# Four microseconds of products between the steps of three delta net lanes in a one-core decoder layer kernel

## The chip, the core and the metric

The kernel runs on one core of one Trainium2 chip. The metric is the device time of one execution, in microseconds (us). Times of a kernel come from a few runs; the profile comes from one execution more.

## What is computed

One layer of a hybrid decoder for 1024 prompt tokens and, with the same weights, 8 x 4 sample tokens, all in float32. A combined projection of the normalised input feeds three branches (sliding-window attention, a short gated convolution, a gated delta net); each branch is projected, gated and summed, and a gated MLP with a convolution follows. The change touches the delta net:

```
q, k = l2norm(q) * dk ** -0.5, l2norm(k)
beta, g = sigmoid(b), -exp(A_log) * softplus(a + dt_bias)
...
a_low = where(strict, (k * beta) @ k.T * decay, 0)
sol = triangular_solve(I + a_low, [v * beta, k * beta * exp(gc)])
qk = q @ k.T * decay
...
v_new = u - w @ S
o = (q * exp(gc)) @ S + qk @ v_new
S = S * exp(glast) + (k * exp(glast - gc)).T @ v_new
```

## The kernel before, in words

**The main line.** The work of TensorE (PE) that matters most is a fixed sequence of jobs of large matmuls, here called products. A projection job takes one block of 128 output columns: for each of three groups of tokens 24 products of 352 columns (`products`, L324), weights and activations split in a high and a low part. An `mm` tile (three PSUM banks in turn) takes each group, and an eviction on ACT or DVE (L1202, L1229, L1252, L1464) frees it. Later jobs are pairs of blocks that share fewer multiplications (`Pairs.run`, L1428, products of 264 columns); the first of them are the gate pairs, G16 and those behind it. Numbers of products in this document count the products in PE's order from the start.

**The lanes.** All else (norms, attention, delta net, their loads and stores) is written as generators, the lanes of class `Lanes` (L84 to L140). Every two to four products the main line calls `tick()`, which moves the clock of the planner by 0.36 to 0.45 us and runs one step of the first lane that is ready. A lane ends a step with a `yield`. A bare `yield` makes it ready at the next turn; `yield bg.after(us)` makes it ready when that many microseconds of products have been emitted; `bg.arrived()` waits for the planned end of its loads. So a lane's `yield` sets how many products stand on PE between a step that computes an operand (on DVE, ACT or POOL) and the matmul that reads it. Afterwards the Tile scheduler puts the instructions of each engine in order by its priorities. Each engine works through its own queue in that order.

**The delta net's lanes.** `pass1` (three lanes share the 8 chunks, L766 to L816) loads a chunk's rows, forms the decay on DVE (L784), ACT and POOL, multiplies on PE (L795) and evicts on DVE (L801, L802). When all chunks are done two lanes start. `solve` inverts the diagonal blocks with 31 pairs of DVE instructions (L827, L829) and a copy (L833); `merge` (L846 to L935) joins the blocks with tiny matmuls (L871, L880 of 32 columns) and lets `prep` and `scan` (L964 to L1011) run over the chunks. `sample_delta` (L1018 to L1126) does the sample group at one go: matmuls L1050, L1057, transposes L1062 to L1064, L1072, L1076, then 32 matmuls L1083 of 8 columns; the evictions L1058, L1059 lie on DVE.

**The gate pairs.** `h_build` (L1811, L1823 on DVE, L1811 on POOL, and splits in a high and a low part by L216 on ACT and L217 on DVE or POOL) makes the combined activations that the gate pairs multiply. Its gate for these is one line, `done.get("prep", 0) == NB and done.get("att", 0) >= HSTART`: all chunks prepared and most of the attention done. It works in four quarters; each product of a combined piece reads all four. `out_norm` (L604, L612) follows the scan.

Of the kernel before, what the change touches and what calls it, by code (L numbers as in the profile page):

```python
# [153 lines left out]
RAWGAP, SUMGAP = 5.0, 10.0  # L154
GAHEAD, GADD, GLO = 4, (), ()
# [14 lines left out]
STEP, EXP, BLKWAIT, PTWAIT, EXP2 = 1.0, 3.0, 4.0, 2.7, 1.0  # L170


def trunk(tc, A, O, cst_d):
    nc = tc.nc
    bg = Lanes()
# [22 lines left out]
    def banks(n):  # L198

        return lambda: held[0] + n <= limit[0]  # L200

    def keep(n):
        held[0] += n
        return [bg_ps() for _ in range(n)]
# [565 lines left out]
    def pass1(c):  # L770
# [18 lines left out]
        yield  # L789
        for hp in range(2):  # L790
            yield banks(1)
            ps, = keep(1)
            for i in range(2):
                h = hp * 2 + i
                mm(ps[:, i * 256:(i + 1) * 256], kn[:, h, :], kq[:, h, :, :].rearrange("p s t -> p (s t)"),  # L795
                   start=True, stop=True)
            yield bg.after(STEP)
            held[0] -= 1
            pv = ps.rearrange("p (h s t) -> p h s t", h=2, s=2)
            hs = slice(hp * 2, hp * 2 + 2)  # L800
            nc.vector.tensor_tensor(At[:, hs, :], pv[:, :, 0, :], Dt[:, hs, :], op=ALU.mult)  # L801
            nc.vector.tensor_tensor(qk[:, hs, :], pv[:, :, 1, :], qk[:, hs, :], op=ALU.mult)  # L802
            yield
# [37 lines left out]
    def merge():  # L841
# [25 lines left out]
        yield bg.arrived()  # L867
        yield banks(1)
# [7 lines left out]
        yield bg.after(1.8)  # L876
# [32 lines left out]
        yield there  # L909
        for i in range(2):  # L910
            yield banks(1)
            ps, = keep(1)
            for g in range(8):
                mm(ps[:, g * 64:g * 64 + 64], A64[i][:, g, :], X64[:, 8 * i + g, :], start=True, stop=True)
                if g % 4 == 3:
                    yield
            held[0] -= 1
            for hh in range(2):
                r = slice(64 * hh, 64 * hh + 64)
                nc.scalar.mul(W64[i][r, :, r], ps[r, :].rearrange("p (g j) -> p g j", j=64), -1.0)  # L920
            yield
# [101 lines left out]
    def sample_delta():  # L1023
# [24 lines left out]
        yield  # L1048
# [6 lines left out]
        yield  # L1055
# [4 lines left out]
        yield  # L1060
# [13 lines left out]
        yield  # L1074
# [18 lines left out]
        yield  # L1093
# [3 lines left out]
        yield  # L1097
# [5 lines left out]
        yield  # L1103
# [1314 lines left out]
```

## Time and profile before

| | us |
|---|---|
| runs, in order | 1893.98, 1896.81, 1889.29 |
| median | 1893.98 |
| profiled execution, its own time | 1890.09 |
| span of that execution | 1888.0 |
| mean granted clock of TensorE in it | 0.968 of full |

The span is the stretch from the first to the last instruction of the profiled execution; the execution's own time is 2.1 us longer. The granted clock is the share of full speed that the chip gave TensorE over the span.

### The profile page before, as it was taken

Reading aid. Unit: us, or ns where it says so; the run is one execution under the profiler, and the core shown is the slowest. Engines: PE = TensorE matmul, PEld = TensorE weight load, DVE = VectorE, ACT = ScalarE, POOL = GpSimd, SP = SyncE. Lnnn points to the kernel's source line nnn. Section 1 sums busy time; section 2 is a strip of 40 time slices with the busy share of each in tenths; the row PEclk is TensorE's granted clock in tenths of the full one; section 3 lists DMA queues with packets and bytes.
Section 4 is the critical chain, followed back from the end, with each engine's and each line's share of the span. In section 5 each row is a group of like instructions: output and inputs, shape, how many; then the busy total and the mean of one; then the engine's idle time right before and its main releaser. Section 6 shows DMA issues by size and latency. Waiting matters only on the chain.

```text
span 1888.0 us, 33612 instructions
## 1 busy us (share of the span) xinstructions
PE 1781.3 (94%) x12862; PEld 1741.7 (92%) x12862; DVE 1127.3 (60%) x1944; ACT 778.3 (41%) x1626; POOL 1061.4 (56%) x985
## 2 busy tenths in 40 slices
PE   5899999898999997999999999999999999899997
PEld 3799988798999996999999999999999999899997
DVE  5578823354478779431234766777777787764324
ACT  5444522221245433444321345445545544454433
POOL 3345534334333329986447246988998988344542
PEclk8899999997999997999999999999999999999999
DMA  6312597656566533553464344444444442695513
GB/s 220 104 47 80 180 301 219 173 154 147 154 163 168 153 104 110 198 207 112 166 223 142 121 137 148 142 153 156 161 147 153 144 161 98 239 369 185 178 48 108
DMA packets 299633, 300.79 MB, mean 159 GB/s; under 512 B 56708, under 2 KB 231280, under 8 KB 299456
## 3 DMA queue, kind: packets, MB, share of 16 engines
q1 hardware_dynamic: 239984, 261.94, 43.3%
q10 hardware_dynamic: 59488, 36.70, 6.8%
q8 instruction: 101, 1.65, 0.4%
q14 instruction: 60, 0.49, 0.1%
HBM read 205.30 MB, written 95.28 MB: 159 GB/s over the span
## 4 chain that ended last, share of the span: by engine, by line
PE 50%; DVE 3%; DMA 2%; ACT 2%; POOL 2%; issue 1%; SPq 0%; DVEq 0%; ACTq 0%; POOLq 0%
PE mm L1428 16%; PE mm L324 12%; PE bgps L1428 12%; PE bgps L2294 2%; PE bgps L2296 2%; PE bgps L2295 2%; PE mm L2295 1%; PE mm L2296 1%; PE mm L2294 1%; DVE slot L2134 1%; DMA slot<-hb_d 1%; DMA wr<-in_ffn_up 1%; DVE slot L2176 1%; DMA st_d<-slot 0%; ACT slot L216 0%
## 5 line engine op out<-in xcount | busy, mean ns | idle before, releaser
L324 PE MATMUL mm<-slot,wh 128*128 128x352 f32 x2496 | 625.3, 331 | 19.6 <-ACT slot L1202 10.9
L324 PEld LDWEIGHTS mm<-slot,wh 128*128 128x128 f32 x2496 | 442.8, 192 | 27.0 <-ACT slot L1202 11.7
L324 PE MATMUL mm<-slot,wl 128*128 128x352 f32 x1248 | 409.7, 328 | 1.9 <-POOL wl L217 1.9
L217 POOL TENSOR_TENSOR wl<-wr,wh 128x1024 fp32r<-128x1024 f32 (+1 forms) x62 | 127.1, 2050 | 233.3 <-ACT wh L216 224.1
L324 PEld LDWEIGHTS mm<-slot,wl 128*128 128x128 f32 x1248 | 239.1, 192 | 4.0 <-POOL wl L217 2.2
L216 ACT CAST slot<-slot 128x528 fp32r<-128x528 f32 (+4 forms) x224 | 143.2, 660 | 129.7 <-DVE slot L1823 27.9
L217 POOL TENSOR_TENSOR slot<-slot 128x512 fp32r<-128x512 f32 (+4 forms) x101 | 148.6, 1478 | 84.6 <-ACT slot L216 77.9
L1428 PE MATMUL mm<-slot,wh 128*128 128x264 f32 x1248 | 172.7, 291 | 17.7 <-ACT slot L1437 8.6
L217 DVE TENSOR_TENSOR slot<-slot 128x528 fp32r<-128x528 f32 (+3 forms) x123 | 130.3, 1073 | 94.2 <-ACT slot L216 87.5
L217 POOL TENSOR_TENSOR wl<-slot,wl 128x512 fp32r<-128x512 f32 x104 | 145.8, 1402 | 71.6 <-ACT wl L216 63.7
L1428 PEld LDWEIGHTS mm<-slot,wh 128*128 128x128 f32 x1248 | 163.0, 194 | 20.8 <-ACT slot L1437 9.9
L217 POOL TENSOR_TENSOR wh<-slot,wh 128x512 fp32r<-128x512 f32 x91 | 122.3, 1343 | 90.6 <-ACT wh L216 74.5
L1428 PE MATMUL mm<-slot,wl 128*128 128x264 f32 x1176 | 155.3, 284 | 0.6 <-ACT slot L1437 0.6
L1428 PEld LDWEIGHTS mm<-slot,wl 128*128 128x128 f32 x1176 | 147.8, 188 | 1.3 <-ACT slot L1437 1.0
L216 ACT CAST wh<-wr 128x512 fp32r<-128x512 f32 (+1 forms) x94 | 75.2, 800 | 161.6 <-PE mm L324 124.1
L2134 DVE SCALAR_TENSOR_TENSOR bgps<-slot,bgps 128x358 f32<-128x358 f32 x240 | 127.3, 588 | 11.8 <-ACT bgps L2132 11.0
L1428 PE MATMUL mm<-slot 128*128 128x264 f32 x936 | 124.5, 284 | 0.7 <-DVE bgps L1456 0.5
L1428 PE MATMUL bgps<-slot,wl 128*128 128x264 f32 x912 | 121.5, 286 | 0.9 <-ACT slot L1437 0.9
L1428 PEld LDWEIGHTS mm<-slot 128*128 128x128 f32 x936 | 118.1, 188 | 1.2 <-DVE bgps L1456 0.7
L1428 PEld LDWEIGHTS bgps<-slot,wl 128*128 128x128 f32 x912 | 116.1, 190 | 1.7 <-ACT slot L1437 1.1
L1428 PE MATMUL bgps<-slot,wh 128*128 128x264 f32 x864 | 113.6, 284 | 1.0 <-ACT slot L1437 0.9
L1428 PEld LDWEIGHTS bgps<-slot,wh 128*128 128x128 f32 x864 | 108.5, 188 | 1.4 <-ACT slot L1437 1.1
(402 smaller groups left out, 3666.9 us busy)
## 6 DMA issues: line engine op xcount, KB each, us to landing
wr<-in_w_in SPq DMA_DIRECT2D x32, 512.0 KB
g_d<-slot SPq DMA_DIRECT2D x24, 528.0 KB
slot<-g_d SPq DMA_DIRECT2D x24, 528.0 KB
ht_d<-slot SPq DMA_DIRECT2D x44, 264.0 KB
slot<-ht_d SPq DMA_DIRECT2D x44, 264.0 KB
wr<-in_ffn_up ACTq DMA_DIRECT2D x22, 512.0 KB
slot<-in_ffn_down SPq DMA_DIRECT2D x22, 512.0 KB
slot<-in_ffn_up ACTq DMA_DIRECT2D x22, 512.0 KB
```

The costliest lines, as they stand in the source:

```text
L216: nc.scalar.copy(hi, src)
L217: eng.tensor_tensor(lo, src, f32(hi), op=ALU.subtract)
L324: mm(ps[:, :TG], a[:, k, :], b[k][:, cc], start=n == 0, stop=n == last)
L1428: mm(ps, w[:, x + k, :], b[y][:, c0:c0 + HU], start=not n and piece not in NESTED, stop=n == last, skip_group_check=piece in NESTED)
L2134: nc.vector.scalar_tensor_tensor(ps, cb[:, a + i:b + i], w(i), ps, op0=ALU.mult, op1=ALU.add)
L2176: sub = lambda out, y, z: nc.vector.tensor_tensor(out, y, z, op=ALU.subtract)
L2294: mm(ps, hi, bh, start=start, stop=False, skip_group_check=True)
L2295: mm(ps, hi, bl, start=False, stop=False, skip_group_check=True)
L2296: mm(ps, lo, bh, start=False, stop=stop, skip_group_check=True)
```

## The change

A constant `LANEGAP = 4.0` comes in. In `pass1`, `merge` and `sample_delta` the `yield` ahead of a matmul that reads what the step before made becomes `yield bg.after(LANEGAP)`: four microseconds of emitted products instead of none (a bare `yield`), of 1.0 (`STEP`) or of 1.8. At two places in `merge` such a `yield` is added behind the wait for loads. No instruction is added, removed or altered; the order of the instructions differs from product 1392 to product 3180 of some 11,400, on every engine. Lines of the changed kernel stand 1 to 4 later than before (L834 for L833, L873 for L871, L1255 for L1252, L1814 for L1811).

```diff
--- before.py
+++ after.py
@@ -152,6 +152,7 @@
 XT_ACT = 0, 2, 4, 6
 AHEADB = 2
 RAWGAP, SUMGAP = 5.0, 10.0
+LANEGAP = 4.0
 GAHEAD, GADD, GLO = 4, (), ()
 DPAHEAD, DPADD, DPLO, DTICK = 3, (1, 2, 3, 4), (0,), 6
 HGAP, HSTART = (0.0, 1.5), 12
@@ -786,7 +787,7 @@
         nc.scalar.activation(flat(Dt), flat(gcb), AF.Exp)
         nc.gpsimd.tensor_tensor(qk, Dt, bch(tri), op=ALU.mult)
         nc.gpsimd.tensor_copy(eD[:, 4 * c:4 * c + 4], Dt[:, :, 127])
-        yield
+        yield bg.after(LANEGAP)
         for hp in range(2):
             yield banks(1)
             ps, = keep(1)
@@ -794,7 +795,7 @@
                 h = hp * 2 + i
                 mm(ps[:, i * 256:(i + 1) * 256], kn[:, h, :], kq[:, h, :, :].rearrange("p s t -> p (s t)"),
                    start=True, stop=True)
-            yield bg.after(STEP)
+            yield bg.after(LANEGAP)
             held[0] -= 1
             pv = ps.rearrange("p (h s t) -> p h s t", h=2, s=2)
             hs = slice(hp * 2, hp * 2 + 2)
@@ -865,6 +866,7 @@
             for i in range(2):
                 dma(Ub[i][r, :, r], xu_d[1][2 * b + 1, eight(hh, i)].rearrange("q i j -> i q j"))
         yield bg.arrived()
+        yield bg.after(LANEGAP)
         yield banks(1)
         ps, = keep(1)
         for g in range(16):
@@ -873,7 +875,7 @@
                 yield
         held[0] -= 1
         nc.scalar.mul(W.rearrange("p g j -> p (g j)"), ps, -1.0)
-        yield bg.after(1.8)
+        yield bg.after(LANEGAP)
         yield banks(1)
         ps, = keep(1)
         for g in range(16):
@@ -907,6 +909,7 @@
         for b, hh, r, gs in four:
             dma(u_d[gs, 64 * b:64 * b + 32, 64 * b + 32:64 * b + 64].rearrange("q j i -> j q i"), U12[r])
         yield there
+        yield bg.after(LANEGAP)
         for i in range(2):
             yield banks(1)
             ps, = keep(1)
@@ -918,7 +921,7 @@
             for hh in range(2):
                 r = slice(64 * hh, 64 * hh + 64)
                 nc.scalar.mul(W64[i][r, :, r], ps[r, :].rearrange("p (g j) -> p g j", j=64), -1.0)
-            yield
+            yield bg.after(LANEGAP)
         for i in range(2):
             yield banks(1)
             ps, = keep(1)
@@ -1045,19 +1048,19 @@
         u4 = lambda t: t.rearrange("p (u t) -> p u t", t=4)
         nc.gpsimd.tensor_copy(kqe[:, :, 0:4], u4(kn))
         nc.gpsimd.tensor_tensor(kqe[:, :, 4:8], u4(q), u4(ebc), op=ALU.mult)
-        yield
+        yield bg.after(LANEGAP)
         ps = bg_ps()
         mm(ps[:, 0:129], G, tri4x, start=True, stop=True)
         nc.scalar.activation(Dt, ps[:, 0:128], AF.Exp)
         nc.scalar.activation(eDs[:, 0:1], ps[:, 128:129], AF.Exp)
         nc.gpsimd.tensor_tensor(B, Dt, su4, op=ALU.mult)
         nc.gpsimd.tensor_tensor(QK, Dt, tri4x[:, 0:128], op=ALU.mult)
-        yield
+        yield bg.after(LANEGAP)
         ps = bg_ps()
         mm(ps[:, 0:256], kn, s1[:, 1:3, :].rearrange("p a b -> p (a b)"), start=True, stop=True)
         nc.vector.tensor_tensor(B, ps[:, 0:128], B, op=ALU.mult)
         nc.vector.tensor_tensor(QK, ps[:, 128:256], QK, op=ALU.mult)
-        yield
+        yield bg.after(LANEGAP)
         ps = bg_ps()
         transpose(ps[:, 0:128], B, ident)
         transpose(ps[:, 128:256], kn, ident)
@@ -1071,7 +1074,7 @@
         ps = bg_ps()
         mm(ps[:, 0:128], As, B, start=True, stop=True)
         nc.vector.tensor_tensor(P, ident, ps[:, 0:128], op=ALU.add)
-        yield
+        yield bg.after(LANEGAP)
         ps = bg_ps()
         mm(ps[:, 0:128], IA, P, start=True, stop=True)
         nc.scalar.copy(U, ps[:, 0:128])
@@ -1090,17 +1093,17 @@
         pv = ps[:, 0:256].rearrange("p (u s) -> p u s", s=8)
         nc.vector.tensor_copy(u4(KST), pv[:, :, 0:4])
         nc.vector.tensor_copy(u4(QST), pv[:, :, 4:8])
-        yield
+        yield bg.after(LANEGAP)
         ps = bg_ps()
         transpose(ps[:, 0:128], KST, ident)
         nc.vector.scalar_tensor_tensor(vb, ps[:, 0:128], nbeg[:, 32:33], vb, op0=ALU.mult, op1=ALU.add)
-        yield
+        yield bg.after(LANEGAP)
         ps = bg_ps()
         mm(ps[:, 0:128], U, vb, start=True, stop=True)
         nc.scalar.copy(vn, ps[:, 0:128])
         nc.vector.tensor_tensor(Vm, vn.unsqueeze(1).to_broadcast([128, 8, 128]),
                                 bm8.unsqueeze(2).to_broadcast([128, 8, 128]), op=ALU.mult)
-        yield
+        yield bg.after(LANEGAP)
         ps = bg_ps()
         mm(ps[:, 0:128], vn, QK, start=True, stop=True)
         nc.vector.tensor_tensor(oTs, ps[:, 0:128], QST, op=ALU.add)
```

The first place is DVE's queue at the end of `solve`. Before the change:

```order
L827 TENSOR_TENSOR slot<-slot 128x31
L829 TENSOR_TENSOR slot<-slot 128x31
L833 COPY slot<-slot 128x32x32
L217 TENSOR_TENSOR slot<-bgps,slot 128x512 x2
L359 SCALAR_TENSOR_TENSOR slot<-slot,vecT 128x1072
L1058 TENSOR_TENSOR slot<-bgps,slot 128x128
L359 SCALAR_TENSOR_TENSOR slot<-slot,vecT 128x1072
L1059 TENSOR_TENSOR slot<-bgps,slot 128x128
```

And with it:

```order
L828 TENSOR_TENSOR slot<-slot 128x31
L830 TENSOR_TENSOR slot<-slot 128x31
L834 COPY slot<-slot 128x32x32
L1255 TENSOR_TENSOR slot<-mm,slot 128x352 x2
L1255 TENSOR_TENSOR slot<-mm,slot 128x320
L1257 TENSOR_TENSOR slot<-mm,slot 128x32
L218 TENSOR_TENSOR slot<-bgps,slot 128x512 x4
L1688 TENSOR_TENSOR slot<-bgps,slot 64x512
L1061 TENSOR_TENSOR slot<-bgps,slot 128x128
L1062 TENSOR_TENSOR slot<-bgps,slot 128x128
```

The solver's last steps and its copy (L833, now L834) stood ahead of L1058, `sample_delta`'s eviction; now they stand ahead of L1252 (now L1255), the evictions of three groups of products, and L1058 (now L1061) comes behind these.

The second place is PE's queue at the tiny matmuls of `sample_delta` and `merge`. Before:

```order
L324 MATMUL mm<-slot,wl 128x352
L1076 MATMUL bgps<-slot 128x128
L1083 MATMUL bgps<-slot 128x8 x16
L1678 MATMUL bgps<-slot 128x512 x4
L871 MATMUL bgps<-slot 128x32 x16
L1083 MATMUL bgps<-slot 128x8 x12
L324 MATMUL mm<-slot,wh 128x352 x2
L880 MATMUL bgps<-slot 128x32 x16
L324 MATMUL mm<-slot,wl 128x352
L324 MATMUL mm<-slot,wh 128x352 x2
```

And with the change:

```order
L1075 MATMUL bgps<-slot 128x128
L873 MATMUL bgps<-slot 128x32 x16
L1079 MATMUL bgps<-slot 128x128
L325 MATMUL mm<-slot,wh 128x352 x2
L325 MATMUL mm<-slot,wl 128x352
L1086 MATMUL bgps<-slot 128x8 x4
L325 MATMUL mm<-slot,wh 128x352 x2
L1086 MATMUL bgps<-slot 128x8 x4
L325 MATMUL mm<-slot,wl 128x352
L325 MATMUL mm<-slot,wh 128x352 x2
L325 MATMUL mm<-slot,wl 128x352
L1086 MATMUL bgps<-slot 128x8 x4
```

The 60 tiny matmuls L1083, L871 and L880 stood together around two products; now L871 (L873) is one run, and L1083 (L1086) and L880 (L882) come by fours with products in between.

The third place is DVE's queue in `h_build` for the gate pairs, near its middle. Before:

```order
L1811 TENSOR_TENSOR slot<-slot 128x1056
L217 TENSOR_TENSOR slot<-slot 128x528
L1823 TENSOR_TENSOR slot<-slot 128x528 x3
L217 TENSOR_TENSOR slot<-slot 128x528
L1823 TENSOR_TENSOR slot<-slot 128x528
L604 TENSOR_TENSOR slot<-slot 128x1056
L217 TENSOR_TENSOR slot<-slot 128x528
L1811 TENSOR_TENSOR slot<-slot 128x1056
L1823 TENSOR_TENSOR slot<-slot 128x528 x3
L217 TENSOR_TENSOR slot<-slot 128x528
L1823 TENSOR_TENSOR slot<-slot 128x528
```

And with the change:

```order
L1826 TENSOR_TENSOR slot<-slot 128x528
L1014 SCALAR_TENSOR_TENSOR slot<-slot,bgps 128x128 x4
L972 TENSOR_TENSOR slot<-bgps,slot 128x512
L973 TENSOR_TENSOR slot<-bgps,slot 128x512
L218 TENSOR_TENSOR slot<-slot 128x528
L1814 TENSOR_TENSOR slot<-slot 128x1056
L994 SCALAR_TENSOR_TENSOR slot<-bgps,slot 128x128 x4
L1014 SCALAR_TENSOR_TENSOR slot<-slot,bgps 128x128 x4
L1826 TENSOR_TENSOR slot<-slot 128x528 x3
L218 TENSOR_TENSOR slot<-slot 128x528
L605 TENSOR_TENSOR slot<-slot 128x1056
L1826 TENSOR_TENSOR slot<-slot 128x528
```

Between the quarters (each begins with L1811, now L1814) there stood one L604 by then; now the last steps of the scan (L1011, L969, L970 and L991, now L1014, L972, L973 and L994) and two L604 (L605) stand there, and more follow.

## Rows read from the trace of the kernel before

**Rows 1.** The page, part 1: busy us (share of the span) x instructions, each engine.
```profile
PE 1781.3 (94%) x12862; PEld 1741.7 (92%) x12862; DVE 1127.3 (60%) x1944; ACT 778.3 (41%) x1626; POOL 1061.4 (56%) x985
```

**Rows 2.** PE's waits, all of the span: us in total, times, longest us.
```profile
PE bgps L1062 <- DVE slot L1058: 6.6, 1, 6.6
...
PE bgps L795 <- DVE slot L802: 5.4, 1, 5.4
...
PE bgps L795 <- DMA slot<-qkv_d: 5.1, 1, 5.1
PE mm L324 <- DVE slot L1464: 3.6, 2, 2.5
...
PE bgps L1751 <- DVE slot L1744: 1.6, 1, 1.6
```

**Rows 3.** Windows: length, busy us (x instructions) by engine, PEclk, DMA share, GB/s.
```profile
440.00:460.00 20.00, 18.74 (x101) 18.35 (x102) 6.37 (x14) 2.64 (x5) 7.87 (x9) 0.67 0.82 177
460.00:480.00 20.00, 20.00 (x99) 20.00 (x100) 2.95 (x5) 2.94 (x5) 5.98 (x4) 0.60 0.72 136
```

**Rows 4.** DVE's timeline about the solver: start us, us, instruction, [idle before <-releaser].
```profile
400.33 0.21 DVE L827 TENSOR_TENSOR slot<-slot 128x31 f32<-128x31 f32 x1
...
437.62 1.03 DVE L833 COPY slot<-slot 128x1024 f32<-128x1024 f32 x1
...
440.92 0.29 DVE L1058 TENSOR_TENSOR slot<-bgps,slot 128x128 f32<-128x128 f32 x1
```

**Rows 5.** PE's timeline, two rows near the start of the gate pairs.
```profile
712.44 0.41 PE L324 MATMUL mm<-slot,wh 128*128 128x352 f32 x1
...
731.72 4.88 PE L1428 MATMUL mm<-slot,wh 128*128 128x264 f32 x24 [6.20 <-ACT slot L1202]
```

**Rows 6.** Windows at the start of the gate pairs, columns as in rows 3.
```profile
720.00:740.00 20.00, 10.39 (x59) 9.89 (x57) 19.68 (x12) 4.80 (x10) 18.69 (x10) 0.80 0.38 136
740.00:760.00 20.00, 16.65 (x94) 15.55 (x95) 18.66 (x10) 10.60 (x20) 19.92 (x12) 0.69 0.42 132
```

**Rows 7.** DVE's timeline while h_build runs for the gate pairs.
```profile
700.02 1.25 DVE L1811 TENSOR_TENSOR slot<-slot 128x1056 f32<-128x1056 f32 x1
701.18 0.68 DVE L1685 TENSOR_TENSOR slot<-bgps,slot 64x512 f32<-64x512 f32 x1
701.79 1.11 DVE L991 SCALAR_TENSOR_TENSOR slot<-bgps,slot 128x128 f32<-128x128 f32 x4
702.82 2.12 DVE L1823 TENSOR_TENSOR slot<-slot 128x528 f32<-128x528 f32 x3
...
712.38 0.94 DVE L1464 SCALAR_TENSOR_TENSOR slot<-slot,mm 128x352 f32<-128x352 f32 x2
...
715.29 1.12 DVE L1011 SCALAR_TENSOR_TENSOR slot<-slot,bgps 128x128 f32<-128x128 f32 x4
...
719.22 1.92 DVE L1811 TENSOR_TENSOR slot<-slot 128x1056 f32<-128x1056 f32 x1
...
730.51 2.31 DVE L604 TENSOR_TENSOR slot<-slot 128x1056 f32<-128x1056 f32 x1
...
738.01 5.09 DVE L1823 TENSOR_TENSOR slot<-slot 128x528 f32<-128x528 f32 x3
...
758.60 2.18 DVE L217 TENSOR_TENSOR slot<-slot 128x1056 fp32r<-128x1056 f32 x1 [1.34 <-ACT slot L216]
```

**Rows 8.** PE's groups by line, 640 to 750 us: busy us, mean ns, idle before.
```profile
L1428 PE MATMUL mm<-slot,wh 128*128 128x264 f32 x48 | 11.5, 418 | 13.0 <-ACT slot L1202 6.2 <-ACT slot L1437 4.9 <-DVE slot L217 1.9
...
L1004 PE MATMUL bgps<-slot 128*128 128x128 f32 x32 | 6.2, 275 | 0.0
...
L996 PE MATMUL bgps<-slot 128*128 128x128 f32 x32 | 4.4, 274 | 0.0
```

## The prediction

> **What bounds the kernel now.** I read the page first, then the waits of PE, then the granted clock by stretch, then the instructions of DVE and PE in three places. PE is busy 94% of the span and no other engine above 60% [rows 1], so a step moved to another place costs or gains nothing in itself: what counts is idle time of PE and time at the lower clock. The reader should look for the lines of the three changed lanes in the list of PE's waits [rows 2]. There are two lines: pass1's L795 (5.4 us behind its own eviction L802, 5.1 us behind the load of qkv_d) and sample_delta's L1062 (6.6 us behind the eviction L1058). Merge does not appear. So the waits that the change aims at are 17.1 us together. The other waits in the region that the change reorders are L1751 with 1.6 us and L324 behind L1464 with 3.6 [rows 2], and at the start of the gate pairs L1428 with 13.0 us: 6.2 behind L1202, 4.9 behind L1437 and 1.9 behind L217 [rows 8].
>
> The second loss is the clock. From 440 to 480 us the granted clock is 0.67 and then 0.60 of full while PE is busy but for 1.3 us [rows 3]. Of the two levels, 2.4 and 1.2 GHz, PE was at the lower one for 2 x (0.33 + 0.40) x 20 = 29 us, and half of it is lost, 14.6 us. What PE did before and in it was the wait of 6.6 us and a pile of tiny matmuls (28 L1083 of 8 columns, 32 of L871 and L880 of 32 columns) with two products and four L1678 among them. I put 3 us of the loss to the wait and 12 to the pile; the rows don't part them.
>
> A product costs 0.16 us at full clock: from product 2944 at 712.44 us to product 3024, held up at 725.52 (731.72 - 6.20), are 80 products in 13.1 us [rows 5].
>
> **The change part by part.** Nothing is added or removed on any engine, so the whole effect is order, from product 1392 to 3180. The sum has five terms.
>
> *pass1.* In the new order the first L795 still stands at product 1392 behind the same load: the 5.1 us stay. The wait behind L802 goes, -5.4. What is late next: L784 of a later chunk stands in DVE's queue ahead of the eviction L1754 of the sample attention and waits itself for a row load. The load that is late in the present order cost 5.4 us; I take 2.4 for the new place. -3; between -8 and +3. The L1751 wait loses its place too, -1.6.
>
> *sample_delta and the solver.* L1062 waited because its operand's eviction L1058 stood in DVE's queue behind the solver: 31 pairs L827, L829 and the copy L833, from 400.33 to 438.65 us, 38.3 us, L1058 only at 440.92 [rows 4]. The change moves L1062 to product 2135, 25 products (4 us) behind L1057, so this wait goes, -6.6. But pass1 now ends later and so does the solver: its last 16 pairs and L833 stand ahead of the first L1252, the eviction of the group that ends at product 2040. There are three mm banks, so product 2089 cannot start before this L1252. The first pair can start when PE is at about product 1957 (behind the eviction of the group that ends at 1944, the last L1638 and an L1642). From there to 2088 PE has 131 x 0.16 = 21 us of products and 17 small matmuls at 0.14 [rows 8], 23.5 us. DVE needs 38.3 less about 2 (9 us of other lines stand among the pairs in the new order, 11 in the old), 36.5. PE waits 13 us: +13 - 6.6 = +6.4, with the clock some more, **+7**. If DVE gets through 10 us sooner there is no wait and the old one is gone, -10 with its clock; if every pair waits for a transfer that is late by 7, +14.
>
> *The pile of tiny matmuls.* The new order puts products in between: L871 in one run of 16, but L1083 and L880 by fours with two products each. From product 2157 to 2176 it is still 48 tiny matmuls beside 19 products, so the clock probably falls, and comes back sooner. I take half of the 12 us: **-6**; between 0 and -12. L871 also needs merge's load of the solver's result; no row shows a wait for it, and the new order leaves 69 products (11 us) and eight L1678 between the solver's end and L871, so nothing is charged.
>
> *Products 2592 to 2950.* The waits on L1464 (3.6) stay in kind: 0, plus or minus 4.
>
> *The gate pairs.* h_build may start only when prep is done with all chunks. The delay adds up over the chain: the last prep transposes move from product 2888 to 3014, the last L996 of scan from 2922 to 3048, and h_build's first L1811 from 2904 to 2988; yet the first product of the gate pairs stays at 3024. That work was not covered before: DVE ran without a gap from 700.02 (first L1811) to 743.10 (the third L1823 of the last quarter) [rows 7], busy 19.7 of 20 us, while PE was busy 10.4 of 20 and 16.7 of 20 us, at clocks of 0.80 and 0.69 [rows 6]. Now the same 43.1 us of DVE start 84 products later. In them, 6.7 us of other lines (L1685, L991, L1464, L1011, L604) were done; in the new order stand L1011 twice, L991, and L969 with L970, priced like them (four times 1.1), three L604 at 2.31 and two L217 of 1056 columns at 2.18, 16 us [rows 7]. One gap comes in where the last chunk's scan goes DVE, PE, ACT, PE, DVE, 16 matmuls and a copy, 4 us. So 43.1 - 6.7 + 16 + 4 = 56 us from product 2988 to the last quarter, where it was 743.10 - 719.5 = 23.6 (product 2988 is 44 products after 712.44). Of the 32.8 us between, PE gets back 44 small matmuls of prep and scan that used to stand before product 2988 (24 at 0.19, the rest near 0.14, 7.4 us [rows 8]), and 24 products of 264 columns (0.12 each) with 12 L612 (0.16), 4.8 us, that it can do in the wait. **+20**. The ends are 0 (the work before 2988 runs ahead of PE) and +30 (DVE slower beside POOL, and the clock).
>
> A dearer price for this term lies in the same rows: they show that DVE is slower beside POOL: three L1823 took 2.12 us at 702.82 and 5.09 us at 738.01 [rows 7]. The first two quarters cost 719.22 - 700.02 = 19.2 us, less 4.4 of other lines, 7.4 each; the last two 23.9, less 2.3, 10.8 each, when POOL was also making the sums of the pairs' weights. The new order gives POOL these sums from product 2988 on, beside all four quarters. If all cost 10.8, the 56 become 43.2 + 16 + 4 = 63, and the term +27.
>
> The Trainium skill, SBUF — State Buffer, section "Who interferes with whom", says that a Vector instruction with both inputs in SBUF shuts out a GpSimd instruction that reads SBUF, and the other way round, for the whole instruction; by that rule the second price holds and the sum is 7 us higher. The rows at 702.82 and 738.01 agree with it, but no row here isolates one pair of instructions.
>
> The sum: -3 - 1.6 + 7 - 6 + 0 + 20 = +16.4 on the profiled execution's 1890.09 us, 1906.5. That execution is 3.9 us below the median of the three runs (1893.98), which themselves lie 7.5 us apart, so I forecast **1906**, 0.6% above the median. From about 760 us on PE has no gap to absorb any of it.
>
> **The rivals.** *Faster, 1860 to 1884:* the named waits go (-5.4, -6.6, -1.6), the clock stays up through the tiny matmuls (-12 and 3), and DVE keeps pace. For it: these are just the waits at the moved lines. Against: DVE's solver is as long as before and starts later. It decides at product 2089: if the solver needs under 24 us from its first pair, it wins there; and h_build must start no later than some 10 us before product 2988. With all of it 1890.1 - 28.6 = 1861.5; with a half, 1876.
>
> *No change, 1886:* the chain to h_build is not later on DVE, because DVE is ahead of PE there; the last term is 0 and the sum -3.6. This is also where it ends if the four microseconds do not separate the steps: the first L795 waits as before, and each wait removed returns at another place.
>
> *Slower still, 1913:* DVE and POOL take turns through all of h_build, the term is +27.
>
> **How the numbers follow.** The measurement tells changes over about 0.5% (9.5 us), that is below 1884.5 or above 1903.5. Forecast 0.42, of which 0.06 end under 1903.5; DVE and POOL in turns 0.12; no change 0.24; faster 0.22. So slower 0.36 + 0.12 = 0.48, same 0.24 + 0.06 = 0.30, faster 0.22. The range goes from 1876 (half of the faster case) to 1928 (1906 with the gate term at its upper end and the solver's at +14, a few us more for the clock). The likeliest case's own range is 1896 to 1920.
>
> **What would show it.** Right: no wait at L1062 and none of 5.4 us at L795; a new wait of L324 behind L1252, of some 13 us, just after the solver's copy L833; a higher clock in the 40 us behind it, with the tiny matmuls in fours; the waits of L1428 at the gate pairs grown from 13 us to some 30, with the last L1823 over 50 us after product 2988. Wrong: no wait at L1252, or L1428's waits at the gate pairs still near 13 us. If the total falls although both are there, the clock was worth more than I gave it.

## The result and the profile after

The changed kernel takes 1919.99 us (median of four runs, 1916.08 to 1923.49); the kernel before takes 1891.78 (four runs, three of them those of the first table). The ratio is 1.0141 with a 95% interval of 1.0125 to 1.0157: 27 us slower. The forecast was 1906 with a range of 1876 to 1928, so direction and range held and the size was about half. In the profiled executions the span grew from 1888.0 to 1914.3 us, by 26.3; the forecast had put 16.4 on the same footing.

The page of the changed kernel, part 1, busy us by engine:

```profile
PE 1787.9 (93%) x12862; PEld 1742.9 (91%) x12862; DVE 1114.8 (58%) x1944; ACT 777.9 (41%) x1626; POOL 1054.4 (55%) x985
```

PE has the same instructions and 7 us more busy time at a share one point lower [rows 1]; part of the rise is time at the lower clock. The list of PE's waits in the changed kernel (total, times, longest; its line numbers are 1 to 3 higher than those of before, and nowhere 4):

```profile
PE mm L325 <- DVE slot L1255: 14.4, 1, 14.4
PE bgps L613 <- ACT slot L217: 12.4, 4, 10.5
...
PE bgps L1764 <- ACT slot L1756: 6.7, 1, 6.7
...
PE bgps L613 <- DVE slot L218: 3.8, 3, 1.9
PE bgps L796 <- DMA slot<-qkv_d: 3.5, 1, 3.5
...
PE bgps L1079 <- DVE slot L1076: 2.3, 1, 2.3
...
PE mm L325 <- DVE slot L1467: 2.1, 2, 1.5
```

L1062's wait of 6.6 us and that of L795 behind L802, 5.4 us, are gone [rows 2], as the change meant. In the first one's place stands the largest wait of the kernel, 14.4 us of the products (L325, before L324) behind the eviction L1255 (before L1252), which the prediction had put at 13. L1764 (before L1761) is the new wait in pass1's stretch, and L613 (before L612), a matmul of `out_norm`, is new at the gate pairs.

The windows of the changed kernel at the two places (columns as in rows 3):

```profile
440.00:460.00 20.00, 5.59 (x37) 5.28 (x36) 18.63 (x44) 3.33 (x7) 4.80 (x7) 0.71 0.25 77
460.00:480.00 20.00, 20.00 (x116) 19.52 (x114) 6.04 (x15) 1.49 (x4) 0.00 (x0) 0.84 0.76 164
480.00:500.00 20.00, 17.70 (x78) 17.57 (x77) 6.74 (x6) 3.45 (x6) 13.54 (x12) 0.50 0.47 101
500.00:520.00 20.00, 20.00 (x111) 19.98 (x111) 1.55 (x4) 2.93 (x5) 4.35 (x3) 0.76 0.37 59
```

```profile
740.00:760.00 20.00, 8.29 (x60) 7.73 (x59) 13.71 (x18) 5.28 (x8) 12.83 (x7) 0.80 0.55 188
760.00:780.00 20.00, 10.92 (x43) 8.40 (x43) 19.59 (x18) 7.46 (x13) 10.37 (x5) 0.51 0.00 0
```

The 20 us from 440 now hold the wait (PE busy 5.6), and the granted clock is at its low of 0.50 from 480 to 500, where the kernel before was back at 1.00; from 440 to 480 before it was 0.67 and 0.60 [rows 3]. At the gate pairs PE is busy 8.3 and 10.9 of 20 us (740 to 780 us), where before it had 10.4 and 16.7 (720 to 760 us) [rows 6].

To compare kernels whose instructions stand in another order I cut PE's time at the same product numbers, and in each section add PE's idle time and half of its busy time at the granted clock of 0.5. Both come from the trace, one execution each. Section 0 to 1380, where all kernels here are the same, varies from 47 to 57 us, so some 5 us of one section in one execution are noise. The sum is an estimate: over the whole span it grows by 25.2 us with the change, where the span grows by 26.3, but in the experiments below it misses the span's growth by between 2 us too much (merge alone) and 8 us too little (the changed kernel with the solver in portions).

| loss in us | 1380-1800 | 2000-2592 | 2592-2960 | 2960-3400 |
|---|---|---|---|---|
| before, idle + clock | 12.3 + 5.1 | 8.0 + 14.0 | 3.8 + 1.7 | 13.0 + 6.5 |
| after | 10.6 + 9.1 | 16.7 + 17.2 | 5.3 + 0.0 | 23.4 + 6.2 |
| difference | +2.3 | +11.9 | -0.2 | +10.1 |
| the prediction's terms | -4.6 | +1 (7 - 6) | 0 | +20 |

The four differences make 24.1 of the 26.3 us. Where the two kernels are the same, the estimate differs by +3.0 (before product 1380) and -1.9 (behind 3400), and 1.1 us stand in no section.

How the solver and the gate pairs look on DVE in the changed kernel (start us, us, instruction, idle before):

```profile
346.62 1.05 DVE L785 TENSOR_SCALAR slot<-slot 128x128 f32<-128x128 f32 x4 [10.14 <-DMA slot<-rows_d]
...
422.09 0.41 DVE L828 TENSOR_TENSOR slot<-slot 128x31 f32<-128x31 f32 x1
...
457.99 1.04 DVE L834 COPY slot<-slot 128x1024 f32<-128x1024 f32 x1
458.87 1.33 DVE L1255 TENSOR_TENSOR slot<-mm,slot 128x352 f32<-128x352 f32 x3
...
728.10 4.20 DVE L1826 TENSOR_TENSOR slot<-slot 128x528 f32<-128x528 f32 x3
...
747.45 1.12 DVE L1014 SCALAR_TENSOR_TENSOR slot<-slot,bgps 128x128 f32<-128x128 f32 x4 [4.12 <-PE bgps L1009]
748.49 2.13 DVE L1826 TENSOR_TENSOR slot<-slot 128x528 f32<-128x528 f32 x3
...
762.50 2.13 DVE L1826 TENSOR_TENSOR slot<-slot 128x528 f32<-128x528 f32 x3
...
774.38 2.13 DVE L1826 TENSOR_TENSOR slot<-slot 128x528 f32<-128x528 f32 x3
```

The solver runs from 422.09 (L828, before L827) to the end of its copy L834 at 459.03: 36.9 us, and L1255 comes right behind. At the gate pairs the third L1826 (before L1823) of the last quarter ends at 776.51.

### The profile page after: what moved, and what is told of

It reads as the page before. It is cut to its first block, busy times and chain, and to the rows that moved or that the text cites. A ratio compares the mean times of both kernels' runs of the same rounds, so it can differ in the third digit from the quotient of the medians.

```text
span 1914.3 us, 33618 instructions
## 1 busy us (share of the span) xinstructions
PE 1787.9 (93%) x12862; PEld 1742.9 (91%) x12862; DVE 1114.8 (58%) x1944; ACT 777.9 (41%) x1626; POOL 1054.4 (55%) x985
## 4 chain that ended last, share of the span: by engine, by line
PE 66%; DVE 12%; DMA 9%; ACT 4%; issue 3%; POOL 3%; SPq 2%; ACTq 0%; DVEq 0%; POOLq 0%
PE mm L325 24%; PE mm L1431 15%; PE bgps L1431 11%; DVE slot L360 2%; SPq L183 2%; PE bgps L2297 2%; PE bgps L2299 2%; PE bgps L2298 2%; DMA wr<-in_w_in 1%; PE mm L2298 1%; PE mm L2299 1%; PE mm L2297 1%; DVE slot L218 1%; DMA slot<-ssq_d 1%; DVE slot L2137 1%
## 5 line engine op out<-in xcount | busy, mean ns | idle before, releaser
L325 PE MATMUL mm<-slot,wh 128*128 128x352 f32 x2496 | 630.6, 333 | 33.7 <-DVE slot L1255 14.4
L325 PEld LDWEIGHTS mm<-slot,wh 128*128 128x128 f32 x2496 | 447.4, 194 | 40.5 <-DVE slot L1255 14.7
L325 PE MATMUL mm<-slot,wl 128*128 128x352 f32 x1248 | 414.2, 332 | 1.3 <-POOL wl L218 1.3
L325 PEld LDWEIGHTS mm<-slot,wl 128*128 128x128 f32 x1248 | 241.6, 194 | 5.5 <-issue 3.2
L1431 PE MATMUL mm<-slot,wh 128*128 128x264 f32 x1248 | 167.6, 286 | 10.0 <-ACT slot L1440 8.5
L218 DVE TENSOR_TENSOR slot<-slot 128x528 fp32r<-128x528 f32 (+3 forms) x123 | 119.8, 989 | 92.8 <-ACT slot L217 86.2
L1431 PEld LDWEIGHTS mm<-slot,wh 128*128 128x128 f32 x1248 | 158.5, 189 | 12.8 <-ACT slot L1440 10.3
L1431 PE MATMUL mm<-slot,wl 128*128 128x264 f32 x1176 | 155.5, 284 | 1.9 <-DVE slot L1493 1.5
L1431 PEld LDWEIGHTS mm<-slot,wl 128*128 128x128 f32 x1176 | 147.9, 188 | 2.6 <-DVE slot L1493 1.7
L2137 DVE SCALAR_TENSOR_TENSOR bgps<-slot,bgps 128x358 f32<-128x358 f32 x240 | 127.2, 589 | 11.2 <-ACT bgps L2135 10.5
L1431 PE MATMUL bgps<-slot,wl 128*128 128x264 f32 x912 | 123.5, 288 | 1.9 <-POOL slot L218 1.1
L1431 PE MATMUL mm<-slot 128*128 128x264 f32 x936 | 124.0, 284 | 0.8 <-DVE bgps L1459 0.6
L1431 PEld LDWEIGHTS bgps<-slot,wl 128*128 128x128 f32 x912 | 117.5, 192 | 3.0 <-POOL slot L218 1.4
L1431 PEld LDWEIGHTS mm<-slot 128*128 128x128 f32 x936 | 117.8, 188 | 1.2 <-DVE bgps L1459 0.8
L1431 PE MATMUL bgps<-slot,wh 128*128 128x264 f32 x864 | 113.7, 284 | 0.9 <-ACT slot L1440 0.9
L1431 PEld LDWEIGHTS bgps<-slot,wh 128*128 128x128 f32 x864 | 108.5, 188 | 1.1 <-ACT slot L1440 1.1
```

The costliest lines, as they stand in the source:

```text
L218: eng.tensor_tensor(lo, src, f32(hi), op=ALU.subtract)
L325: mm(ps[:, :TG], a[:, k, :], b[k][:, cc], start=n == 0, stop=n == last)
L1431: mm(ps, w[:, x + k, :], b[y][:, c0:c0 + HU], start=not n and piece not in NESTED, stop=n == last, skip_group_check=piece in NESTED)
L2137: nc.vector.scalar_tensor_tensor(ps, cb[:, a + i:b + i], w(i), ps, op0=ALU.mult, op1=ALU.add)
```

## The experiments

Eleven kernels ran, each timed in five rounds beside the kernel before. `LANEGAP` is the change's constant. Losses are those of the table above, idle plus clock.

| kernel | ratio to before, 95% | 1380-1800 | 2000-2592 | 2592-2960 | 2960-3400 |
|---|---|---|---|---|---|
| before | 1 | 17.4 | 22.0 | 5.5 | 19.5 |
| changed kernel | 1.0141 (1.0125-1.0157) | 19.7 | 33.9 | 5.3 | 29.6 |
| pass1 alone | 1.0041 (1.0028-1.0054) | 19.2 | 27.6 | 3.4 | 22.1 |
| merge alone | 1.0047 (1.0034-1.0060) | 16.6 | 22.7 | 0.0 | 33.9 |
| sample_delta alone | 1.0014 (1.0004-1.0024) | 16.2 | 28.5 | 0.7 | 21.6 |
| changed, early h_build | 1.0110 (1.0094-1.0126) | 17.0 | 33.5 | 5.2 | 18.8 |
| changed, tiny matmuls in piles | 1.0168 (1.0148-1.0188) | 19.0 | 29.4 | 12.3 | 30.6 |
| changed, solver in portions | 1.0046 (1.0028-1.0064) | 18.2 | 5.9 | 1.8 | 43.5 |
| before, early h_build | 0.9987 (0.9974-0.9999) | 17.8 | 25.1 | 5.5 | 15.9 |
| before, solver by fours, early h_build | 0.9962 (0.9950-0.9975) | 17.6 | 18.9 | 0.0 | 11.7 |
| changed with 2 us | 1.0023 (1.0011-1.0035) | 14.4 | 21.3 | 5.6 | 25.8 |
| before, solver by twos, early h_build | 0.9938 (0.9924-0.9952) | 16.6 | 20.7 | 1.0 | 15.6 |
| solver by fours, early h_build, sample_delta's gap | 0.9943 (0.9929-0.9956) | 16.4 | 16.0 | 0.0 | 18.3 |

**The three lanes one by one.** The first takes only the two hunks of the diff in pass1, the second those in merge, the third those in sample_delta.

```diff
-        yield
+        yield bg.after(LANEGAP)
...
-            yield bg.after(STEP)
+            yield bg.after(LANEGAP)
```

> The gap of 4 us in pass1 alone; merge and sample_delta as before. Theory A (each lane does its own harm: pass1 makes the solver late): the solver's copy L833 again stands ahead of the first L1252 at product 2088, so the wait behind it is there with 12 to 16 us, while h_build starts at product 2914 instead of 2904, so the gate pairs lose nothing new: 18 us over the kernel before, about 1910. Rival B (the harm comes from the gaps in merge and sample_delta): no more than 4 us over it. Rival C (the late gate pairs are the larger part): no more than 8 us.

Measured: 1897.97 us, a ratio of 1.0041, 7.7 us. The wait is there, and the gate pairs are nearly as before:

```profile
PE mm L325 <- DVE slot L1253: 14.9, 1, 14.9
...
PE bgps L1762 <- ACT slot L1754: 5.2, 1, 5.2
```

So the gap in pass1 makes this wait by itself, as theory A had it, 14.9 us. But it costs 5.6 us in its section, not the 12 that the changed kernel loses there. Theory A had the mechanism and more than twice the price; by its bound rival C stands better, but the gate pairs are not the larger part in the change either (table above).

```diff
         yield bg.arrived()
+        yield bg.after(LANEGAP)
         yield banks(1)
...
-        yield bg.after(1.8)
+        yield bg.after(LANEGAP)
...
         yield there
+        yield bg.after(LANEGAP)
...
-            yield
+            yield bg.after(LANEGAP)
```

> The gap in merge alone. The solver stands where it stood; h_build's first L1811 moves from product 2904 to 2983. Theory A (merge makes h_build late, and only that): the wait of L1062 stays with 6 to 7 us, nothing at L1252, and idle time between products 2988 and 3200 grows from 13 to 20 to 25 us: 10 us over the kernel before, 1902. Rival (h_build's late start is covered): within 3 us of the kernel before. My forecast of the gate pairs alone, taken literally, would give 20 us, 1912.

Measured: 1899.45 us, 1.0047, 8.9 us. The wait of L1062 (here L1065) stays, no wait at L1252, and the gate pairs lose 33.9 us in place of 19.5:

```profile
PE bgps L613 <- ACT slot L217: 12.9, 4, 10.9
...
PE bgps L1065 <- DVE slot L1061: 6.8, 1, 6.8
```

That is theory A. The term of 20 us for the gate pairs, taken literally, is too high.

```diff
-        yield
+        yield bg.after(LANEGAP)
```

(seven times in sample_delta)

> The gap in sample_delta alone. In its order 16 L871 of merge stand ahead of L1062 at product 2055, and need the solver and its loads. Theory A: PE waits there until about 15 us after the solver's copy L833, some 18 us where L1062 cost 6.6; h_build starts at 2883, no loss at the gate pairs: 12 to 15 us over the kernel before, 1905. Rival (the gap does for sample_delta what it says, L1062's wait goes and its time is won): 5 to 10 us under the kernel before.

Measured: 1892.40 us, 1.0014, 2.6 us. PE's timeline there, all rows with an idle time between 428 and 452 us:

```profile
438.27 0.80 PE L1679 MATMUL bgps<-slot 128*128 128x512 f32 x1 [8.59 <-DVE slot L218]
...
449.95 2.31 PE L872 MATMUL bgps<-slot 128*128 128x32 f32 x10 [5.30 <-DMA slot<-xu_d]
```

L1062's wait went. In its place a transposed value for L1678 (here L1679) waits 8.6 us for an eviction that stands behind the solver's copy, and L871 (here L872) waits 5.3 us for merge's load. I had put 18 us at L871 alone; 13.9 came in two pieces. The total shows neither the theory's 12 us nor the rival's gain: the wait moved on, and cost 6.5 us in its section.

By the ratios the three parts cost 7.7, 8.9 and 2.6 us, 19 together; the change costs 27. The sections don't tell where the other 8 us arise: between products 2000 and 2592 the parts lose 5.6, 0.7 and 6.5 us more than before, the change 11.9; at the gate pairs 2.6, 14.4 and 2.1, the change 10.1. In all three parts the stretch from 2592 to 2960 was 2 to 5.5 us better than before, in the change it was not. That is the size of one trace's noise, so it stays open.

**The start of h_build.** The gate line with 6 of 8 chunks, in the changed kernel and then in the kernel before:

```diff
-            yield lambda: done.get("prep", 0) == NB and done.get("att", 0) >= HSTART
+            yield lambda: done.get("prep", 0) >= NB - 2 and done.get("att", 0) >= HSTART
```

> The changed kernel with one edit: h_build for the gate pairs may start when prep has done 6 of 8 chunks, so that its first L1811 stands at product 2933 instead of 2988. Theory (the late start costs the 10 us that the two traces differ by between products 2592 and 3400): idle time at the gate pairs falls from 23 us to 13 or less, 1908 to 1912. Rival (DVE and POOL are full in either order, and the start does not matter): within 3 us of the changed kernel, 1920.

Measured: 1909.83 us, 1.0110. Beside the change's 1.0141 that is 6 us by the ratios (10 by the medians), but the two intervals touch, so the total alone does not rule out the rival's 3 us. The loss at the gate pairs does: it falls from 29.6 to 18.8 us, that of before, and no other section of the table moves by more than 3 us. The late start is a cause of the loss there; DVE and POOL are not simply full.

> The kernel before with the one edit on h_build's start (prep done with 6 of 8 chunks): its last L1811 moves from product 3046 to 3002, the last L1823 from 3060 to 3024. Theory (the gate pairs wait for h_build, in the kernel before too): idle time and clock loss at the gate pairs fall from 19.5 us to about 10, 8 to 10 us under the kernel before, 1881. Rival (DVE and POOL are full, an earlier start is worth nothing): within 3 us of it.

Measured: 1887.96 us, 0.9987: the interval ends at 0.9999, 2.5 us. The loss at the gate pairs falls by 3.6 us, not by 8 to 10. Before the change most of this loss is not the start's; the rival is nearer.

**The block of the solver.**

```diff
-            if j % 8 == 7:
-                yield
+            if j % 4 == 3:
+                yield bg.after(LANEGAP)
```

> The changed kernel with the solver's 31 pairs emitted by fours, each four microseconds of products behind the last. Theory E (the wait at L1252 is the solver's block in DVE's queue, not a lack of DVE time): the wait of 14.4 us falls under 3, and idle time with clock loss between products 2000 and 2200 from 32 us to 10 to 18. Rival (DVE is simply full there): the wait stays above 10 us. The solver ends 84 products later and h_build starts at 3024, so the gate pairs lose 5 to 15 us more than the changed kernel's 30; the total is 1912 to 1925.

Measured: 1898.97 us, 1.0046, some 18 us under the changed kernel. Waits and windows of this kernel:

```profile
PE bgps L613 <- ACT slot L217: 11.3, 3, 10.0
...
PE mm L325 <- DVE slot L1255: 0.8, 1, 0.8
```

```profile
440.00:460.00 20.00, 19.21 (x120) 18.65 (x119) 19.39 (x43) 4.49 (x8) 8.62 (x10) 0.94 0.40 108
460.00:480.00 20.00, 20.00 (x117) 20.00 (x117) 13.92 (x36) 6.11 (x21) 8.76 (x7) 0.81 0.75 172
```

The wait at L1252 (here L1255) is 0.8 us, where it was 14.4, and DVE is still busy 19.4 of 20 us from 440 to 460: DVE is as full as before and PE no longer waits for it, so what held PE was the order of DVE's queue and not a lack of DVE time. The section's loss falls from 33.9 to 5.9 us, which shows theory E; I had expected 10 to 18. The gate pairs lose 14 us more, as h_build starts later, at the upper end of what was expected. The total lies 13 us under the range that I had given (1912 to 1925). The profiled execution, 1905.14 us, is the slowest of this kernel's nine, so its sections may be too high.

**The tiny matmuls.**

```diff
             mm(ps[:, g * 32:g * 32 + 32], A[g // 8][:, g % 8, :], X11[:, g, :], start=True, stop=True)
-            if g % 4 == 3:
-                yield
...
-            if u % 4 == 3:
-                yield there if u == 15 else None
+            if u == 15:
+                yield there
```

> The changed kernel without the yields between the tiny matmuls of sample_delta and merge (L1083, L871, L880), so that they stand on PE in four runs instead of by fours between products. Theory D (by fours they keep PE at the lower clock longer than in one pile): time at the lower clock between products 2000 and 2592 falls from 48 us in the changed kernel to about 34, as in the kernel with pass1's gap alone, 5 to 7 us of loss less there. Rival (the 14 us wait sets that clock, not the tiny matmuls): 45 us or more as before. h_build starts 22 products later (3010), which may cost up to 5 us of it again, so the total is 1912 to 1920.

Measured: 1922.52 us, 1.0168. Windows of this kernel over the same 80 us:

```profile
440.00:460.00 20.00, 5.81 (x34) 5.52 (x32) 18.70 (x45) 3.33 (x7) 5.00 (x7) 0.69 0.24 80
460.00:480.00 20.00, 17.21 (x112) 16.68 (x110) 5.26 (x13) 2.79 (x5) 0.00 (x0) 0.93 0.70 144
480.00:500.00 20.00, 18.74 (x106) 18.75 (x107) 7.02 (x7) 3.20 (x7) 13.55 (x12) 0.70 0.47 108
500.00:520.00 20.00, 20.00 (x133) 19.98 (x131) 2.79 (x6) 2.14 (x4) 6.36 (x5) 0.91 0.63 105
```

The wait is the same, but from 480 to 520 the clock is 0.70 and 0.91 where the changed kernel had 0.50 and 0.76. Between products 2000 and 2592 the trace has 34.1 us at the lower clock against 47.8: theory D's number. Two more traces agree: 44.4 us with the same fours (changed kernel, early h_build) and 34.1 with runs (pass1 alone), both behind the same kind of wait (14.3 and 14.9 us). The 7 us of clock loss saved there (10.1 against 17.2) were partly spent on more idle time (19.3 against 16.7), and products 2592 to 2960 lost 7 more; the total is above the expected range, and its interval overlaps that of the change. So the runs of tiny matmuls are shown to shorten the time at the lower clock, not the kernel. With the solver in portions most tiny matmuls (all but a first run of 12) also stand by fours, farther apart and without a long wait ahead of them, and only 10.2 us are at the lower clock. So fours between products are not bad in themselves; which of the wait and the spacing decides was not tried alone.

**Half the gap**, in all three lanes.

```diff
-LANEGAP = 4.0
+LANEGAP = 2.0
```

> The changed kernel with a gap of 2 us in place of 4 in all three lanes. The solver then ends where it ended in the kernel before (its copy at product 2016, ahead of a job that ACT evicts) and h_build starts at 2914. Theory (the 4 us cost by where the solver and h_build come to stand, not by the gaps as such): no wait at L1252, one of 4 to 8 us at L1062 (product 2049); between products 2000 and 2200 a loss of 20 to 26 us as before, at the gate pairs 20 to 24: 1890 to 1896. Rival (cost in proportion to the gap): half of the change's 27 us, 1904.

Measured: 1893.41 us, 1.0023, 4.4 us: the theory, not half of 27. The solver stands where it stood before the change, and PE waits for it at L1062 (here L1065), longer than I said:

```profile
PE bgps L1065 <- DVE slot L1061: 13.5, 1, 13.5
```

The loss of the section, 21.3 us, is that of before; the gate pairs lose 25.8, above the 24 expected. The cost is a matter of where the blocks land, and does not follow the gap in proportion.

**Versions that beat both.** None of the three lanes is touched; the solver comes in portions and h_build starts at 6 of 8 chunks.

```diff
-            if j % 8 == 7:
-                yield
+            if j % 4 == 3:
+                yield bg.after(LANEGAP)
...
-            yield lambda: done.get("prep", 0) == NB and done.get("att", 0) >= HSTART
+            yield lambda: done.get("prep", 0) >= NB - 2 and done.get("att", 0) >= HSTART
```

> The kernel before, none of the three lanes changed, with the solver's pairs by fours (four microseconds of products between) and h_build's start at 6 of 8 chunks. Theory: what hurts both kernels is the solver's block in DVE's queue and h_build's late start. L1062 then stands at product 1997, ahead of most of the solver, and its 6.6 us wait goes; the tiny matmuls come apart (L1083 at 2016 to 2043, L871 at 2210); the loss between 2000 and 2200 falls from 22 us to 8 to 12, that at the gate pairs from 19.5 to 10 to 15: 1872 to 1880, under both kernels. Rival (the waits move on to the next eviction): 1885 to 1892.

Measured: 1883.04 us, 0.9962. L1062's wait is gone, but one of 6.0 us at L1076 (the sample group's next step behind L1073) takes its place; the gate pairs lose 11.7 us. Faster than both kernels, by 7 us and not by 10 to 18: the rival had a part.

With portions of two pairs and the same edit on h_build's start:

```diff
-            if j % 8 == 7:
-                yield
+            if j % 2 == 1:
+                yield bg.after(2.0)
```

> The kernel before with h_build's start at 6 of 8 chunks and the solver's pairs by twos, two microseconds of products between (the kernel with fours and 4 us gave 1883). The sample group's evictions then find a gap in DVE's queue after two pairs instead of four: the wait behind L1073 of 6.0 us falls under 3, the clock loss with it: 1876 to 1881. Rival (that wait is a chain of POOL and ACT work, not DVE's queue): 1882 to 1885, the wait as it was.

Measured: 1877.65 us, 0.9938. The total is in the expected range and the reason is wrong: the wait is still there, as the rival said.

```profile
PE bgps L1077 <- DVE slot L1074: 6.0, 1, 6.0
```

Where the 5 us against the version by fours come from, the sections do not tell: 20.7 against 18.9 us and 15.6 against 11.7 are losses, and the gain lies behind product 3400, 22.0 against 28.1, where both are the same. It is measured and not explained.

With portions of four, the same edit on h_build's start, and the change's seven gaps in sample_delta:

```diff
-            if j % 8 == 7:
-                yield
+            if j % 4 == 3:
+                yield bg.after(4.0)
...
-        yield
+        yield bg.after(LANEGAP)
```

> The kernel with the solver's pairs by fours and h_build's start at 6 of 8 chunks, and with the change's gap in sample_delta alone. If the gap is worth what it is for once the solver does not block DVE, no wait of the sample group's chain (L1062, L1072, L1076) is left between products 2000 and 2200, idle there under 2 us against 6.0. But the gate pairs start later (2934 instead of 2894, prep's last at 3048), 3 to 8 us: 1880 to 1888 together.

Measured: 1877.63 us, 0.9943. Idle time between products 2000 and 2200 falls to 4.4 us, not under 2, because the wait at L1076 is still there with 3.7 us; the gate pairs lose 6.6 us more than without the gap, as expected. The total is 2 us under the range that I had given. So once the solver does not block DVE, the change's idea in this lane costs nothing and may be worth 3 to 4 us (0.9943 against 0.9962, intervals that overlap at the edge).

## Why the prediction was right in direction and short in size

*pass1, -4.6 forecast, +2.3 measured.* The waits of 5.4 and 1.6 us went, and the load behind the first L795 stayed, as said. The term failed in the new wait: sized at 2.4 us, it measured 6.7, with 4 us more of clock. The +2.3 of one trace is within its noise, but no gain of 4.6 is there: five traces with pass1's gap of 4 us lose 17.0 to 19.7 us in this section, seven without it 16.2 to 17.8. The late load was named rightly, the way to PE only in part. L784 (L785 in the changed kernel) waits 10.14 us on DVE for its row load [the row at 346.62 above]. The prediction put DVE's copy L1754 behind it; PE's wait ended with ACT's copy L1756 (before L1753), because ACT's queue stands behind L785 as well:

```profile
347.70 0.63 ACT L787 ACTIVATE slot<-slot 128x512 f32<-128x512 f32 x1 [11.82 <-DVE slot L785]
348.24 0.35 ACT L1756 COPY slot<-bgps 128x256 f32<-128x256 f32 x1
```

The load was issued at 340.19 us, in the kernel before at 330.35, because SP had the stores of two chunks ahead of it:

```profile
328.41 1.95 SPq L183 DMA_DIRECT2D blk_d<-slot  x4
330.40 1.89 SPq L183 DMA_DIRECT2D a_d<-slot  x3
...
333.04 1.83 SPq L183 DMA_DIRECT2D blk_d<-slot  x4
334.91 1.86 SPq L183 DMA_DIRECT2D a_d<-slot  x3
...
340.19 0.98 SPq L183 DMA_DIRECT2D slot<-rows_d  x2
```

The prediction took half the price of the late load before the change; that two chunks now finish together and put their stores in front of the next load was not seen. With pass1's gap alone the same stores and the same wait are there (5.2 us). The late load itself was not tried alone; this cause is read from the traces.

*The solver, +7.* Right in every step. The start (product 1957; the trace has it at 421.94, the first L827 at 422.09), the length (forecast 36.5, measured 36.9), PE's time from there to product 2088 (23.5; 23.1) and the wait (13; 14.4). The runs of pass1 alone and of the solver in portions show the cause: pass1 moves the block, the block makes the wait. In all versions with an undivided block PE waits for it: 6.6 us at L1062 before, 14.4 at the product behind the eviction L1252 with the change, 8.6 at L1678 with sample_delta's gap alone, 13.5 at L1062 with 2 us. What changes is who stands behind it.

*The tiny matmuls, -6.* This gain did not come. Clock loss from product 2000 to 2592 went from 14.0 to 17.2 us and did not fall by 6; the rise itself is within what one trace varies by (the order of before gives 14.0 and 17.3 us in two traces, that of the change 17.2 and 15.8). The prediction said that the products between the tiny matmuls would bring the clock back sooner; behind the same wait the piles give 10.1 and, with pass1's gap alone, 11.6, so beside them the spacing that the change brought has the opposite sign. One mark that the prediction set itself, a higher clock in the 40 us behind the solver's copy, is hardly there: 0.84 and 0.50 from 460 to 500 us, where the 40 us from 440 before had 0.67 and 0.60 [rows 3]. The second wait, L1076 behind L1073 (2.3 us), was not forecast either. With the solver's term this section was put at +1 and measured +11.9: here is the larger part of the shortfall.

*The gate pairs, +20.* That a late start of h_build costs time is right, as merge alone (+14.4 in the section) and the early start (back to 18.8) show; the term is twice too large, +10.1, and the matmul that waits is another than the one named. The prediction had the waits of L1428 grow from 13 us to some 30. L1431 (before L1428) waits only 5.6 us there, and L613 (before L612), which sums squares for `out_norm`, 14.7:

```profile
757.90 0.53 PE L613 MATMUL bgps<-slot,hot 128*48 128x352 f32 x1 [10.49 <-ACT slot L217]
...
775.54 2.35 PE L1431 MATMUL mm<-slot,wh 128*128 128x264 f32 x9 [4.51 <-ACT slot L1440]
```

L613 stands ahead of the next pairs in PE's queue. Its operand comes from L605 (before L604), which stands in DVE's queue behind the scan's last L1014 and the three L1826 at 748.49 [rows above], and waits 2.0 us for a load of its own:

```profile
754.34 1.26 DVE L605 TENSOR_TENSOR slot<-slot 128x1056 f32<-128x1056 f32 x1 [1.99 <-DMA slot<-o_d]
```

With the early start L613 waits 1.3 us and L1431 8.4. How much of the 10.5 us is h_build's and how much the scan's and its load's was not tried alone.

The third L1826 of the last quarter ended 776.51 - 728.77 = 47.7 us after product 2988, not 56. The gap for the scan was there with 4.1 us (forecast 4). What was dearer in the forecast is a quarter of h_build. Three L1826 took 4.20 us once and then 2.13 three times; before, three L1823 took 2.12 and 5.09 in the first and the last quarter [rows 7] and these in the two between:

```profile
713.24 2.13 DVE L1823 TENSOR_TENSOR slot<-slot 128x528 f32<-128x528 f32 x3
...
723.95 3.23 DVE L1823 TENSOR_TENSOR slot<-slot 128x528 f32<-128x528 f32 x3
```

The prediction had POOL make the sums of the pairs' weights beside all four quarters. In the trace the last of them (L1394, from 743.39) ended at 744.65, ahead of the three that took 2.13 us, and at each of these POOL had been idle, waiting for ACT:

```profile
749.93 3.56 POOL L218 TENSOR_TENSOR slot<-slot 128x528 fp32r<-128x528 f32 x2 [4.05 <-ACT slot L217]
...
763.94 3.59 POOL L218 TENSOR_TENSOR slot<-slot 128x528 fp32r<-128x528 f32 x2 [4.26 <-ACT slot L217]
...
776.09 1.59 POOL L218 TENSOR_TENSOR slot<-slot 128x528 fp32r<-128x528 f32 x1 [4.54 <-ACT slot L217]
```

So the dearer rival at 1913, by which DVE and POOL take turns through all quarters, fell with its condition. The Trainium skill (SBUF — State Buffer, "Who interferes with whom") says that a Vector instruction with two inputs in SBUF contends with a GpSimd instruction that reads SBUF. The trace agrees: the 4.20 us stand where POOL was busy 18.6 of 20 us, the 2.13 us where it was mostly idle; still no row isolates a pair.

*The total.* On the spans the forecast missed by 9.9 us: 6.9 in pass1, 10.9 in the solver's and the tiny matmuls' section, less 9.9 at the gate pairs, and 2 in stretches that the change does not touch. Errors of both signs hid each other in part, so that the total came within the range is in part luck. Of the two rivals on the other side, "faster" needed a solver of under 24 us from its first pair, and "no change" needed h_build in time; neither held.

## What to carry to other kernels

A gap that is measured in products of the main line does not only loosen one wait: it delays everything that the lane's end releases, here a long block of DVE work and the start of the operands for a later stage. Before putting gaps in, look for the long blocks in an engine's queue and ask whose eviction stands behind each of them in the new order; to divide the block cured the wait (14.4 to 0.8 us) where moving it only changed the victim. Then follow the chain to the next gate, and price the start of what lies behind it.

## What was not expected of the hardware

With 64 tiny matmuls, 48 of them by fours with products between, PE was at a granted clock of 0.5 for longer (47.8 us between products 2000 and 2592) than with the same matmuls in four runs (34.1 us), both behind a wait of 14 us; with most fours farther apart and no such wait it was 10.2 us. PE was busy in most of that time (34.4 of the 47.8 us), so a busy engine is no sign of a full clock.
